# Seven block products instead of eight for three more pairs of column chunks per layer, in a two-layer hybrid mixer

## The chip, the cores and the metric

The kernel runs on one core of one Trainium2 chip. The metric is the device time in microseconds (us). Three runs of the kernel before took 2103.38, 2103.51 and 2104.88 us; their median is 2103.51 us.

## The reference, cut to what matters

Each of two layers multiplies the 256 tokens (width 2048) by one wide matrix `w_in`, splits the result into the inputs of four branches A, B, C, D and the gates, runs four attentions, and merges. All is float32.

```python
for l in range(DEPTH):                                   # 2 layers
    h = jnp.einsum('bsd,de->bse', x, w_in[l])            # 256 tokens x 2048 -> D_IN columns
    (aq, ak, av, az, bq, bk, bv, bz, cq, ck, cv, cz, dq, dk, dv, dz, gl) = _split(h, IN_SIZES)
    ya, yb, yc, yd = ...                                 # differential, neighbourhood, axial GQA, dilated attention
    ys = jnp.stack([ya * silu(az), yb * silu(bz), yc * silu(cz), yd * silu(dz)], axis=2)
    proj = jnp.einsum('bsnw,nwd->bsnd', ys, w_branch[l])
    gates = sigmoid(gl + b_gate)                         # 4 branches x 2048 columns
    merged = jnp.sum(proj * gates, axis=2)
    x = layer_norm(ALPHA * x + merged @ w_out[l])
```

## The kernel before

**Products.** The transposed activations lie in SBUF (the core's working memory) as a high part `th` and a low part `tl` (both in the tile `tx`). Weights come by DMA in groups of two 128-row blocks (`load_raw`, L140), and are split into a high part by ScalarE (`whi`, L150) and a low part by VectorE (`wlo`, L151). Each block product is three matmuls: low times high, high times high, high times low. `whl` holds four groups of split weights, so the splits can run up to some groups ahead of TensorE.

**Chunks.** `chunk` (L195 to L199) multiplies all 2048 rows by one chunk of up to 512 columns: eight groups of two blocks, each for both halves of the tokens, 12 matmuls a group and 96 a chunk. `chunk_t` (L222, L223) makes a part of 256 columns transposed, 64 matmuls in four groups; branch D's queries and keys come that way, two parts to a call of `pairs`. After a part, `fold` copies one half of each sum out of PSUM (the accumulator banks) on ScalarE (`fo`, L231) and adds the other on VectorE (L235), and `rotate` applies the rotary factors: two copies on ScalarE (`xs`, L330), three operations on VectorE (L332 to L334). `xs` lies in a scratch tile with the tag `rb`.

**Seven products.** The gate columns already go by pairs of chunks. For the first four of the 16 row blocks, taken as a 2x2 arrangement (two token halves by two groups of rows) against two groups of rows by two chunks, `gate_pair` makes the result from seven block products instead of eight. It needs sums of activations, `sh` and `sl`, which `quarter_sums` makes once per layer: a sum `xq` (tag `ra`), four sums `xf` (tag `rb`), and their split into `sh` (ScalarE) and `sl` (VectorE). It also adds raw weights to each other (L864), and keeps partial results in `keep` (tag `ra`) and `part` (tag `rb`). It uses all four banks of the pool `psw`.

**Order.** `step()` advances the attention tasks by one stage after every group, so their small matmuls (scores `sc`, transposes `pt`, values `po`) lie between the groups. In a layer: columns of A, `quarter_sums`, columns of B, gates of branch 0, columns of C (chunk `Cz`, then two units `Cqkv0` and `Cqkv1`), gates of branch 1, columns of D, gates of branches 2 and 3, output product. In D each head's values (`Dv0` to `Dv3`, 384 columns) come after the queries and keys it needs, and the head's attention is queued after its values. The framework sets each engine's order when the program is built; on the chip each engine goes through its list in order.

Of the kernel before, what the change touches and what calls it, by code (L numbers as in the profile page):

```python
# [17 lines left out]
P = 128  # L18
# [76 lines left out]
def hybrid_encoder(ctx: ExitStack, tc: tile.TileContext, a: dict, out: bass.AP):  # L95
# [579 lines left out]
    for l in range(DEPTH):  # L675
# [45 lines left out]
        def cols_t(nm, part):  # L721
            return chunk_t(w_in, OFFSETS[nm] + part * D * TCH)

        def v_tile():
            return att.tile([P, 1024], F32, tag="v", name="v")[:, :768].rearrange("p (t n) -> p t n", t=2)

        def columns_ab(br):
            zs, ysT = new_branch()
            for u in range(2):
                v = v_tile()  # L730
                first = (br, u) == ("A", 0)
                if first and l == 0:
                    with tc.manual_schedule(engines={mybir.EngineType.PE, mybir.EngineType.Activation, mybir.EngineType.DVE, mybir.EngineType.SP}):
# [8 lines left out]
                        sw.extend(small_weights())  # L742
                neglam, sg, gn, bias = sw
                for half in range(2):
                    nc.vector.tensor_copy(v[:, half, 0:256], ps[half][:, 0:256])
# [15 lines left out]

        def columns_c():
            zs, ysT = new_branch()
            ps = cols("Cz")
            for half in range(2):
                silu2(ps[half], zs[:, half])
            for u in range(2):
                qk, v = qkT_tile(3, F32).rearrange("p (t n) -> p t n", t=2), v_tile()
                ps = cols(f"Cqkv{u}")
                for half in range(2):  # L770
                    nc.scalar.copy(qk[:, half, 0:384], ps[half][:, 0:384])
                    nc.vector.tensor_copy(v[:, half, 0:128], ps[half][:, 384:512])
                tasks.append(attend_c(u, qk, v, zs, ysT, sw[2]))
            return ysT

        def columns_d():
            zs, ysT = new_branch()
            mask_d = cst.tile([P, 768], F32, tag="bias", name="mask_d")
            nc.sync.dma_start(out=mask_d, in_=a["mask_d"])
            ps = cols("Dz", True)  # L780
            for half in range(2):
                silu2(ps[half], zs[:, half])
            table = [rope_d[:, i].unsqueeze(1).to_broadcast([64, 2, 2, P]) for i in range(2)]
            ready = []
# [12 lines left out]
            heads = []  # L797
            for h in range(4):
                while len(ready) < 3 * h + 3:
                    pairs(len(ready) // 2)  # L800
                v = v_tile()
                for half, ps in enumerate(cols(f"Dv{h}", True)):
                    nc.vector.tensor_copy(v[:, half], ps)
                tasks.append(attend_d(h, heads[h], v, zs, ysT, mask_d))
            return ysT

        def merged_t(c):
# [9 lines left out]
            merged_t(3)  # L817
            yield

        def quarter_sums():  # L820
# [4 lines left out]
            (a11, a12), (a21, a22) = ([x[:, j * KG:(j + 1) * KG, i * P:(i + 1) * P] for j in range(2)] for i in range(2))  # L825
# [4 lines left out]
        def product(bank, lh, ll, w, start=False, stop=False):  # L830

            hi, lo = w
            for k in range(KG):
                nc.tensor.matmul(bank, lhsT=ll[k], rhs=hi[:, k], start=start and k == 0, stop=False, skip_group_check=True)  # L834
                nc.tensor.matmul(bank, lhsT=lh[k], rhs=hi[:, k], start=False, stop=False, skip_group_check=True)  # L835
            for k in range(KG):
                nc.tensor.matmul(bank, lhsT=lh[k], rhs=lo[:, k], start=False, stop=stop and k == KG - 1, skip_group_check=True)  # L837

        def plain(half, g):
            return [[tok(t, g * KG + k, half, False) for k in range(KG)] for t in (th, tl)]  # L840

        def summed(i):
            return [[t[:, i, k] for k in range(KG)] for t in (sh, sl)]

        def gate_pair(b, cp):


            c1, c2 = 2 * cp + 1, 2 * cp
            bgs = []
            for c in (c1, c2):  # L850
# [3 lines left out]
            bg1, bg2 = bgs  # L854
            size = P * KG * NCH

            def raw(c, g):
                return load_raw(w_in, OFFSETS[f"G{b}{c}"] + g * size, KG * NCH)

            def bank():  # L860
                return psw.tile([P, NCH], F32, tag="pw", name="pw")

            def add(out, x, y, op=ALU.add):
                nc.vector.tensor_tensor(out=out, in0=x, in1=y, op=op)  # L864

            def gate(t):
                g = vec.tile([P, NCH], F32, tag="g", bufs=3, name="g")
                nc.scalar.activation(out=g, in_=t, func=AF.Tanh, scale=0.5)
                return g

            def tmp():
                return vec.tile([P, NCH], F32, tag="tmp", bufs=3, name="gt")

            def rest(c, g, p0, p1, first=False):

                w = split_w(raw(c, g), NCH)
                product(p1, *plain(1, g), w, first, g == NK // KG - 1)
                product(p0, *plain(0, g), w, False, g == NK // KG - 1)
                step()

            keep = att.tile([P, 2, NCH], F32, tag="ra", name="keep", bufs=1)
            part = att.tile([P, 2, NCH], F32, tag="rb", name="part", bufs=1)
            r11, r12, r21 = raw(c1, 0), raw(c2, 0), raw(c1, 1)
            pa = bank()
            product(pa, *plain(0, 0), split_w(r11, NCH), True)
            add(r11, r11, r12)
            add(keep[:, 0], pa, bg1)
            pd = bank()
            product(pd, *summed(0), split_w(r11, NCH), True)
            add(keep[:, 1], pd, bg2)  # L890
            pb = bank()
            product(pb, *plain(0, 1), split_w(r21, NCH), True)
            step()
            r22 = raw(c2, 1)
            pe = bank()
            rest(c2, 2, pd, pe, True)
            add(r11, r11, r22)
            product(pa, *summed(1), split_w(r11, NCH))
            add(part[:, 0], pa, bg2, ALU.subtract)
            step()  # L900
            rest(c2, 3, pd, pe)
            add(r12, r12, r22)
            product(pa, *summed(2), split_w(r12, NCH))
            add(part[:, 1], pa, keep[:, 1], ALU.subtract)
            rest(c2, 4, pd, pe)
            add(r11, r11, r21)
            product(pa, *plain(1, 1), split_w(r11, NCH))
            step()
            rest(c2, 5, pd, pe)
            product(pd, *summed(3), split_w(r22, NCH))  # L910
            rest(c2, 6, pd, pe)
            rest(c2, 7, pd, pe)
            ts = [tmp(), tmp()]
            add(ts[1], pe, part[:, 1], ALU.subtract)
            add(ts[0], pd, part[:, 0], ALU.subtract)
            gs = [gate(t) for t in ts]
            rest(c1, 2, pb, pa)
            rest(c1, 3, pb, pa)
            yield gs
            for g in range(4, NK // KG):  # L920
                rest(c1, g, pb, pa)
            ts = [tmp(), tmp()]
            add(ts[1], pa, bg1)
            add(ts[0], pb, keep[:, 0])
            yield [gate(t) for t in ts]

        def gates(b, ysT, first):
            yh, yl = ysT
# [15 lines left out]
                            nc.vector.tensor_tensor(out=merged[:, half, cs], in0=merged[:, half, cs], in1=t, op=ALU.add)  # L944

        pending = {}

        def drain_for(b):
            want = pending.pop(b)
# [146 lines left out]
```

## Time and profile before

| | |
|---|---|
| median of 3 runs | 2103.51 us |
| the profiled execution | 2104.6 us, of which the span of the program is 2102.8 us |
| TensorE matmuls (PE) | 2084.4 us busy, 99% of the span, 10384 matmuls |
| TensorE weight loads (PEld) | 1767.7 us, 84% |
| VectorE (DVE) | 1479.4 us, 70% |
| ScalarE (ACT) | 1045.7 us, 50% |
| GpSimd (POOL) | 38.3 us, 2% |
| DMA | 410.78 MB, mean 195 GB/s |
| share of PE in the chain that ended last | 96% |

Busy time is the union of an engine's instructions. A matmul's own duration is longer than its turn on the engine, since matmuls overlap: the turn is read from the distance of their starts in the timeline. The time of a timeline row with several instructions runs from the first one's start to the last one's end.

### The profile page before, as it was taken

The numbers are of one execution on the slowest core, as the hardware profiler recorded it, in microseconds if no ns is written. First come the engines' busy times: TensorE is split into PE (matmuls) and PEld (weight loads), VectorE is DVE, ScalarE is ACT, GpSimd is POOL, SyncE is SP. The second block draws the span as 40 slices with busy tenths as digits, with TensorE's granted clock in tenths as the row PEclk, the third lists the DMA queues.
The fourth block names the chain that finished last, engine by engine and source line by source line (L and its number), as shares of the span: only waits on it lengthen the run. The fifth ranks groups of instructions, "written<-read, shape, count | busy, mean of one in ns | idle before, by whom it ended". The sixth has DMA issues, their size and how long they took to land.

```text
span 2102.8 us, 27473 instructions
## 1 busy us (share of the span) xinstructions
PE 2084.4 (99%) x10384; PEld 1767.7 (84%) x10384; DVE 1479.4 (70%) x1823; ACT 1045.7 (50%) x1385; POOL 38.3 (2%) x34
## 2 busy tenths in 40 slices
PE   8999999999999999999999999999999999999997
PEld 6888888888898988888888888888889999888886
DVE  6777775877666677776676777657766666777766
ACT  6664554544555554444446545445445454544542
POOL 2000000000000010000000000000000000000000
PEclk9999999999999999999999999999999999999999
DMA  8567666556555566666665545755655554666664
GB/s 272 170 197 239 203 201 199 190 186 213 161 181 164 177 229 207 220 211 216 201 216 180 173 142 189 243 188 191 205 189 181 176 162 149 220 210 215 212 212 126
DMA packets 121603, 410.78 MB, mean 195 GB/s; under 512 B 13888, under 2 KB 14912, under 8 KB 120960
## 3 DMA queue, kind: packets, MB, share of 16 engines
q1 hardware_dynamic: 120608, 407.98, 59.6%
q8 instruction: 81, 1.33, 0.3%
q10 hardware_dynamic: 864, 1.07, 0.2%
q14 instruction: 50, 0.41, 0.1%
HBM read 402.70 MB, written 6.29 MB: 195 GB/s over the span
## 4 chain that ended last, share of the span: by engine, by line
PE 96%; DVE 1%; DMA 1%; ACT 0%; issue 0%; SPq 0%; ACTq 0%; DVEq 0%
PE pw L222 14%; PE pw L195 12%; PE pw L196 12%; PE pw L199 12%; PE pw L837 11%; PE pw L834 11%; PE pw L835 11%; PE pw L223 7%; PE pt L296 1%; PE po L451 1%; PE po L523 1%; PE sc L509 1%; DVE wlo L151 0%; PE sc L383 0%; DMA lnr<-in_emb_ln_g 0%; PE pt L812 0%
## 5 line engine op out<-in xcount | busy, mean ns | idle before, releaser
L151 DVE TENSOR_TENSOR wlo<-wraw,whi 128x1024 fp32r<-128x1024 f32 (+1 forms) x768 | 917.0, 1203 | 486.0 <-ACT whi L150 482.0
L150 ACT CAST whi<-wraw 128x1024 fp32r<-128x1024 f32 (+1 forms) x768 | 789.6, 1033 | 871.2 <-PE pw L196 301.9
L222 PE MATMUL pw<-tx,whi 128*128 128x512 f32 x1280 | 458.0, 401 | 0.0
L195 PE MATMUL pw<-whi,tx 128*128 128x512 f32 (+1 forms) x944 | 358.1, 379 | 0.4 <-DVE tx L241 0.4
L223 PE MATMUL pw<-tx,wlo 128*128 128x256 f32 x1280 | 358.4, 280 | 0.0
L196 PE MATMUL pw<-whi,tx 128*128 128x512 f32 (+1 forms) x944 | 354.5, 376 | 0.0
L834 PE MATMUL pw<-whi,tx 128*128 128x512 f32 x864 | 339.0, 392 | 0.0
L835 PE MATMUL pw<-whi,tx 128*128 128x512 f32 x864 | 336.6, 390 | 0.0
L222 PEld LDWEIGHTS pw<-tx,whi 128*128 128x128 f32 x1280 | 240.4, 188 | 55.2
L199 PE MATMUL pw<-wlo,tx 128*128 128x512 f32 (+1 forms) x944 | 277.9, 375 | 0.0
L837 PE MATMUL pw<-wlo,tx 128*128 128x512 f32 x864 | 265.9, 390 | 0.0
L223 PEld LDWEIGHTS pw<-tx,wlo 128*128 128x128 f32 x1280 | 241.7, 189 | 0.4
L195 PEld LDWEIGHTS pw<-whi,tx 128*128 128x128 f32 x944 | 179.3, 190 | 27.4 <-DVE tx L241 0.6
L196 PEld LDWEIGHTS pw<-whi,tx 128*128 128x128 f32 x944 | 179.3, 190 | 25.8
L199 PEld LDWEIGHTS pw<-wlo,tx 128*128 128x128 f32 x944 | 176.4, 190 | 27.5
L837 PEld LDWEIGHTS pw<-wlo,tx 128*128 128x128 f32 x864 | 161.3, 188 | 36.2 <-DVE wlo L151 2.1
L834 PEld LDWEIGHTS pw<-whi,tx 128*128 128x128 f32 x864 | 162.3, 188 | 32.8
L835 PEld LDWEIGHTS pw<-whi,tx 128*128 128x128 f32 x864 | 162.3, 188 | 32.8
L195 PE MATMUL pw<-whi,yl 128*128 128x512 f32 x256 | 100.2, 391 | 0.0
L196 PE MATMUL pw<-whi,yh 128*128 128x512 f32 x256 | 99.7, 389 | 0.0
L199 PE MATMUL pw<-wlo,yh 128*128 128x512 f32 x256 | 79.5, 391 | 0.0
L864 DVE TENSOR_TENSOR wraw<-wraw 128x1024 f32<-128x1024 f32 x64 | 78.0, 1219 | 0.8
(174 smaller groups left out, 1660.1 us busy)
## 6 DMA issues: line engine op xcount, KB each, us to landing
wraw<-in_w_in SPq DMA_DIRECT2D x544, 512.0 KB, 4.2
wraw<-in_w_branch SPq DMA_DIRECT2D x64, 512.0 KB, 4.8
wraw<-in_w_out SPq DMA_DIRECT2D x64, 512.0 KB, 4.3
wraw<-in_w_in SPq DMA_DIRECT2D x64, 384.0 KB, 3.1
bg<-in_b_gate SPq DMA_DIRECT2D x32, 256.0 KB, 4.9
xr<-x_dram SPq DMA_DIRECT2D x16, 256.0 KB, 4.7
bias<-in_rpb SPq DMA_DIRECT2D x2, 1024.0 KB, 7.2
x_dram<-merged SPq DMA_DIRECT2D x8, 256.0 KB, 4.9
```

The lines of the kernel that those rows point to most:

```text
L150: nc.scalar.copy(hi[:, :w], raw)
L151: nc.vector.tensor_tensor(out=lo[:, :w], in0=raw, in1=hi[:, :w].bitcast(F32), op=ALU.subtract)
L195: nc.tensor.matmul(acc[half][:, :n], lhsT=tok(ll, k, half, perm), rhs=hi[:, kk, :n], start=k == 0, stop=False)
L196: nc.tensor.matmul(acc[half][:, :n], lhsT=tok(lh, k, half, perm), rhs=hi[:, kk, :n], start=False, stop=False)
L199: nc.tensor.matmul(acc[half][:, :n], lhsT=tok(lh, k, half, perm), rhs=lo[:, kk, :n], start=False, stop=k == nkt - 1)
L222: nc.tensor.matmul(acc[b], lhsT=hi[:, kk, cs], rhs=tx[:, k].rearrange("p h t -> p (h t)"), start=k == 0, stop=False)
L223: nc.tensor.matmul(acc[b][:, SEQ:], lhsT=lo[:, kk, cs], rhs=th[:, k, :], start=False, stop=k == NK - 1)
L296: nc.tensor.transpose(pt[:, q * P:(q + 1) * P], src[:, q * P:(q + 1) * P], ident)
L834: nc.tensor.matmul(bank, lhsT=ll[k], rhs=hi[:, k], start=start and k == 0, stop=False, skip_group_check=True)
L835: nc.tensor.matmul(bank, lhsT=lh[k], rhs=hi[:, k], start=False, stop=False, skip_group_check=True)
L837: nc.tensor.matmul(bank, lhsT=lh[k], rhs=lo[:, k], start=False, stop=stop and k == KG - 1, skip_group_check=True)
L864: nc.vector.tensor_tensor(out=out, in0=x, in1=y, op=op)
```

## The change

Three more pairs of chunks per layer go through the seven products: `Cz` with `Cqkv0`, `Dv0` with `Dv1`, and `Dv2` with `Dv3`. The body of `gate_pair` becomes `seven`, with the bias as an option; without one, three evacuations per pair are ScalarE copies instead of VectorE additions (`kept`, L880 of the new file). Branch D takes its token halves as even and odd tokens, so the sums are made anew in that order at the start of D (`quarter_sums(True)`), and back in the plain order at its end (`quarter_sums()`). `drain_to(1)` advances the queued attention until one task is left. The values of a pair of heads now come together, after the queries and keys of the first of them. Calls before in D: pairs 0, 1, `Dv0`, pairs 2, `Dv1`, pairs 3, 4, `Dv2`, pairs 5, `Dv3`. Calls now: sums, pairs 0, 1, `Dv0` and `Dv1`, pairs 2, pairs 3, 4, `Dv2` and `Dv3`, pairs 5, sums. What follows in both is the gates of branch 2.

```diff
 def columns_c():
-    ps = cols("Cz")
+    both = cols_pair("Cz", "Cqkv0")
+    ps = next(both)
...
-        ps = cols(f"Cqkv{u}")
+        ps = cols("Cqkv1") if u else next(both)
 def columns_d():
+    quarter_sums(True)
     ps = cols("Dz", True)
...
     for h in range(4):
         while len(ready) < 3 * h + 3:
             pairs(len(ready) // 2)
-        v = v_tile()
-        for half, ps in enumerate(cols(f"Dv{h}", True)):
-            nc.vector.tensor_copy(v[:, half], ps)
-        tasks.append(attend_d(h, heads[h], v, zs, ysT, mask_d))
+        if h % 2 == 0:
+            both = cols_pair(f"Dv{h}", f"Dv{h + 1}", True)
+            vs = []
+        for ps in both:
+            drain_to(1)
+            vs += v_tiles(1, 384)
+            for half in range(2):
+                nc.vector.tensor_copy(vs[-1][:, half], ps[half])
+            if h % 2 == 0 and len(vs) == 1:
+                tasks.append(attend_d(h, heads[h], vs[0], zs, ysT, mask_d))
+        if h % 2:
+            tasks.append(attend_d(h, heads[h], vs[1], zs, ysT, mask_d))
+    quarter_sums()
     return ysT
 -def quarter_sums():
+def quarter_sums(perm=False):
...
+def seven(raw, n, perm=False, bias=None):
...
+    def kept(out, x, i, op=ALU.add):
+        if bias:
+            add(out, x, bias[i], op)
+        else:
+            nc.scalar.copy(out, x)
...
+    r11, r12, r21 = raw(1, 0), raw(0, 0), raw(1, 1)
+    pa = bank()
+    product(pa, *plain(0, 0), split_w(r11, n), True)
+    add(r11, r11, r12)
+    kept(keep[:, 0], pa, 1)
+    pd = bank()
+    product(pd, *summed(0), split_w(r11, n), True)
+    kept(keep[:, 1], pd, 0)
+    pb = bank()
+    product(pb, *plain(0, 1), split_w(r21, n), True)
...
```

**First place: TensorE where branch D ends and the gates of branch 2 begin, layer 0.** Before, the last chunk is `Dv3`; `pw_6651` and `pw_6664` are the banks of the gate pair's first and second product, `pw_6676` that of the third, and `sc_6687` holds head 3's first scores.

```order
L199 MATMUL pw_6480<-wlo_6622,tx_98 128x384 x2
...
L835 MATMUL pw_6651<-whi_6652,tx_98 128x512
L837 MATMUL pw_6651<-wlo_6653,tx_98 128x512 x2
...
L834 MATMUL pw_6664<-whi_6665,sl_101 128x512
L835 MATMUL pw_6664<-whi_6665,sh_100 128x512
L837 MATMUL pw_6664<-wlo_6666,sh_100 128x512 x2
...
L837 MATMUL pw_6676<-wlo_6678,tx_98 128x512 x2
L509 MATMUL sc_6687<-qkT_6068 128x256
L509 MATMUL sc_6687<-qkT_6068 128x128 x2
```

Now the last matmuls of D are those of the last part of pairs 5 (bank `pw_6577`). `pw_6710`, `pw_6723` and `pw_6735` are the first, second and third product's banks, `sc_6746` head 3's first scores, `pt_6792` the transposes of its softmax.

```order
L223 MATMUL pw_6577<-tx_98,wlo_6659 128x256
...
L863 MATMUL pw_6710<-whi_6711,tx_98 128x512
L865 MATMUL pw_6710<-wlo_6712,tx_98 128x512 x2
L509 MATMUL sc_6746<-qkT_6099 128x256
L509 MATMUL sc_6746<-qkT_6099 128x128 x2
L296 MATMUL pt_6792<-ident_87,pr_6754 128x128 x4
L862 MATMUL pw_6723<-whi_6724,sl_101 128x512
L863 MATMUL pw_6723<-whi_6724,sh_100 128x512
...
L865 MATMUL pw_6735<-wlo_6737,tx_98 128x512 x2
```

The scores and the transposes moved ahead of the second product, and the 96 matmuls of `Dv3` that stood between pairs 5 and the gates are gone from there. Layer 1 has the same order.

**The same place on VectorE.** Before, from the copy of the last values on:

```order
L803 COPY v_6478<-pw_6480 128x384
L864 TENSOR_TENSOR keep_6643<-pw_6651,bg_6639 128x512
L151 TENSOR_TENSOR wlo_6706<-wraw_6703,whi_6705 128x1024
L864 TENSOR_TENSOR keep_6643<-pw_6664,bg_6641 128x512
L864 TENSOR_TENSOR wraw_6645<-wraw_6645,wraw_6700 128x1024
L512 SCALAR_TENSOR_TENSOR scb_6691<-sc_6687,mask_d_4399 128x512
L283 TENSOR_REDUCE nm_6693<-scb_6691 128x1
```

Now, from the second-last split before the rotation of pairs 5's last part (`qkT_6099`) to the low part of the sums, which the second product reads:

```order
L151 TENSOR_TENSOR wlo_6782<-wraw_6704,whi_6781 128x1024
L874 TENSOR_TENSOR wraw_6704<-wraw_6704,wraw_6708 128x1024
L332 TENSOR_TENSOR qkT_6099<-qkT_6099,rope_d_94 64x512
L333 TENSOR_TENSOR xs_6683<-xs_6683,rope_d_94 64x512
L334 TENSOR_TENSOR qkT_6099<-qkT_6099,xs_6683 64x512
L848 TENSOR_TENSOR xf_6690<-xq_6689 128x256 x2
L848 TENSOR_TENSOR xf_6690<-xf_6690,xq_6689 128x256
L512 SCALAR_TENSOR_TENSOR scb_6750<-sc_6746,mask_d_4402 128x512
L848 TENSOR_TENSOR xf_6690<-xf_6690,xq_6689 128x256
L283 TENSOR_REDUCE nm_6752<-scb_6750 128x1
L874 TENSOR_TENSOR keep_6702<-pw_6710,bg_6700 128x512
L241 TENSOR_TENSOR sl_101<-xf_6690,sh_100 128x1024
```

The rotation, the four sums, the softmax of head 3 and the evacuation of the first product stand in one line ahead of `sl_101`, none of which was there before.

**Second place: ScalarE where `Dv2` begins, layer 0.** Before: `fo` and `xs` belong to the last part of pairs 4, the casts to 768 columns are `Dv2`'s.

```order
L231 COPY fo_5967<-pw_5865 128x256
L150 CAST whi_6048<-wraw_6046 128x1024
L231 COPY fo_5967<-pw_5866 128x256
L330 COPY xs_5972<-qkT_5725 32x512 x2
L150 CAST whi_6085<-wraw_6083 128x768
L150 CAST whi_6103<-wraw_6101 128x768
```

Now, with `keep` from the first (`pw_6119`) and the second product (`pw_6132`):

```order
L231 COPY fo_6100<-pw_6009 128x256
L150 CAST whi_6160<-wraw_6158 128x768
L231 COPY fo_6100<-pw_6010 128x256
L150 CAST whi_6177<-wraw_6113 128x768
L880 COPY keep_6111<-pw_6119 128x384
L150 CAST whi_6190<-wraw_6188 128x768
L330 COPY xs_6105<-qkT_6099 32x512 x2
L880 COPY keep_6111<-pw_6132 128x384
```

The copies of the first products out of PSUM are new on ScalarE here, and the second one stands behind two casts and the rotation's copies. Where `Dv0` begins, and in layer 1, the order is the same.

## Rows read from the trace of the kernel before

**Rows 1.** The page: busy time of TensorE, and the chain by engine.
```profile
PE 2084.4 (99%) x10384; PEld 1767.7 (84%) x10384; DVE 1479.4 (70%) x1823; ACT 1045.7 (50%) x1385; POOL 38.3 (2%) x34
...
PE 96%; DVE 1%; DMA 1%; ACT 0%; issue 0%; SPq 0%; ACTq 0%; DVEq 0%
```
**Rows 2.** Timeline, TensorE, `Dv0` of layer 0, first and last (start us, us, instruction).
```profile
575.57 0.34 PE L195 MATMUL pw<-whi,tx 128*128 128x384 f32 x1
...
591.87 0.51 PE L199 MATMUL pw<-wlo,tx 128*128 128x384 f32 x2
```
**Rows 3.** Timeline, TensorE, the output chunks of layer 0, first and last.
```profile
969.87 0.48 PE L195 MATMUL pw<-whi,tx 128*128 128x512 f32 x1
...
1053.85 0.62 PE L199 MATMUL pw<-wsp,tx 128*128 128x512 f32 x2
```
**Rows 4.** Groups by form: busy us, mean ns, idle before.
```profile
L834 PE MATMUL pw<-whi,tx 128*128 128x512 f32 x864 | 339.0, 392 | 0.0
...
L290 ACT ACTIVATE pr<-scb,nm 128x512 f32<-128x512 f32 x16 | 11.6, 723 | 28.5 <-DVE nm L283 28.5
...
L512 DVE SCALAR_TENSOR_TENSOR scb<-sc,mask_d 128x512 f32<-128x512 f32 x16 | 11.0, 689 | 11.2 <-PE sc L509 11.1
...
L771 ACT COPY qkT<-pw 128x384 f32<-128x384 f32 x8 | 3.8, 477 | 2.9 <-PE pw L199 2.9
```
**Rows 5.** Timeline, three engines, end of pairs 5 in layer 0.
```profile
727.41 0.28 PE L223 MATMUL pw<-tx,wlo 128*128 128x256 f32 x1
...
727.65 0.83 ACT L150 CAST whi<-wraw 128x768 fp32r<-128x768 f32 x1 [0.94 <-PE pw L222]
...
728.87 0.38 ACT L231 COPY fo<-pw 128x256 f32<-128x256 f32 x1
...
729.40 0.42 DVE L235 TENSOR_TENSOR qkT<-pw,fo 128x256 f32<-128x256 f32 x1
...
729.85 1.25 ACT L330 COPY xs<-qkT 32x512 f32<-32x512 f32 x2 [0.60 <-DVE qkT L235]
...
731.13 0.68 DVE L332 TENSOR_TENSOR qkT<-qkT,rope_d 64x512 f32<-64x512 f32 x1 [1.31 <-ACT xs L330]
...
732.34 0.94 DVE L151 TENSOR_TENSOR wlo<-wraw,whi 128x768 fp32r<-128x768 f32 x1
...
733.21 0.68 DVE L334 TENSOR_TENSOR qkT<-qkT,xs 64x512 f32<-64x512 f32 x1
```
**Rows 6.** Timeline, the shortest rotation in D and the longest in A.
```profile
552.28 0.28 PE L223 MATMUL pw<-tx,wlo 128*128 128x256 f32 x1
...
557.34 0.67 DVE L334 TENSOR_TENSOR qkT<-qkT,xs 64x512 f32<-64x512 f32 x1
...
65.12 0.28 PE L223 MATMUL pw<-tx,wlo 128*128 128x256 f32 x1
...
73.74 0.69 DVE L334 TENSOR_TENSOR xr<-xr,xs 128x512 f32<-128x512 f32 x1
```
**Rows 7.** Timeline, VectorE and ScalarE, the sums of layer 0 after branch A.
```profile
125.94 1.22 DVE L824 TENSOR_TENSOR xq<-tx 128x1024 f32<-128x1024 f32 x1
...
127.19 0.76 DVE L827 TENSOR_TENSOR xf<-xq 128x256 f32<-128x256 f32 x2
...
129.86 1.05 ACT L240 CAST sh<-xf 128x1024 fp32r<-128x1024 f32 x1
...
131.14 1.22 DVE L241 TENSOR_TENSOR sl<-xf,sh 128x1024 fp32r<-128x1024 f32 x1
```
**Rows 8.** Stretches at the end: us, busy us (instructions) of each engine, granted clock, DMA.
```profile
2091.50:2095.00 3.50, 0.28 (x2) 0.00 (x0) 3.08 (x7) 0.00 (x0) 0.99 (x1) 1.00 0.00 0
2095.00:2099.00 4.00, 0.00 (x0) 0.00 (x0) 4.00 (x7) 0.00 (x0) 0.00 (x0) 0.51 0.37 131
```
**Rows 9.** Stretches at the start, the transposes into the tile idle alone (TensorE, weight loads).
```profile
1.34:5.34 4.00, 4.00 (x19) 4.00 (x20) 1.00 0.77 228
6.34:8.34 2.00, 1.92 (x18) 1.68 (x16) 1.00 1.10 363
```

More of the change, by code (lines that the diff above doesn't have):

```diff
@@ L722, in cols_t, with v_tiles, cols_pair @@
             return chunk_t(w_in, OFFSETS[nm] + part * D * TCH)
-        def v_tile():
-            return att.tile([P, 1024], F32, tag="v", name="v")[:, :768].rearrange("p (t n) -> p t n", t=2)
+        def v_tiles(units, n):
+            v = att.tile([P, 1024], F32, tag="v", name="v")
+            return [v[:, u * 2 * n:(u + 1) * 2 * n].rearrange("p (t n) -> p t n", t=2) for u in range(units)]
+        def cols_pair(one, other, perm=False):
+            n = len(CHUNKS[one])
+            return seven(lambda i, g: load_raw(w_in, OFFSETS[(one, other)[i]] + g * P * KG * n, KG * n), n, perm)
         def columns_ab(br):
@@ L828, in quarter_sums @@
             split_evac(sh, sl, f)
[L830 to L843, printed above, removed]
+        def seven(raw, n, perm=False, bias=None):
+            def bank():
+                return psw.tile([P, NCH], F32, tag="pw", name="pw")[:, :n]
+            def product(bank, lh, ll, w, start=False, stop=False):
+                hi, lo = w
+                for k in range(KG):
+                    nc.tensor.matmul(bank, lhsT=ll[k], rhs=hi[:, k], start=start and k == 0, stop=False, skip_group_check=True)
+                    nc.tensor.matmul(bank, lhsT=lh[k], rhs=hi[:, k], start=False, stop=False, skip_group_check=True)
+                for k in range(KG):
+                    nc.tensor.matmul(bank, lhsT=lh[k], rhs=lo[:, k], start=False, stop=stop and k == KG - 1, skip_group_check=True)
+            def plain(half, g):
+                return [[tok(t, g * KG + k, half, perm) for k in range(KG)] for t in (th, tl)]
+            def summed(i):
+                return [[t[:, i, k] for k in range(KG)] for t in (sh, sl)]
+            def add(out, x, y, op=ALU.add):
+                nc.vector.tensor_tensor(out=out, in0=x, in1=y, op=op)
+            def kept(out, x, i, op=ALU.add):
[3 more added lines that the diff above has]
+                    nc.scalar.copy(out, x)
+            def rest(i, g, p0, p1, first=False):
+                w = split_w(raw(i, g), n)
+                product(p1, *plain(1, g), w, first, g == NK // KG - 1)
+                product(p0, *plain(0, g), w, False, g == NK // KG - 1)
+                step()
+            keep = att.tile([P, 2, NCH], F32, tag="ra", name="keep", bufs=1)[:, :, :n]
+            part = att.tile([P, 2, NCH], F32, tag="rb", name="part", bufs=1)[:, :, :n]
+            r11, r12, r21 = raw(1, 0), raw(0, 0), raw(1, 1)
[8 more added lines that the diff above has]
+            product(pb, *plain(0, 1), split_w(r21, n), True)
+            step()
+            r22 = raw(0, 1)
+            pe = bank()
+            rest(0, 2, pd, pe, True)
+            add(r11, r11, r22)
+            product(pa, *summed(1), split_w(r11, n))
+            kept(part[:, 0], pa, 0, ALU.subtract)
+            step()
+            rest(0, 3, pd, pe)
+            add(r12, r12, r22)
+            product(pa, *summed(2), split_w(r12, n))
+            add(part[:, 1], pa, keep[:, 1], ALU.subtract)
+            rest(0, 4, pd, pe)
+            add(r11, r11, r21)
+            product(pa, *plain(1, 1), split_w(r11, n))
+            step()
+            rest(0, 5, pd, pe)
+            product(pd, *summed(3), split_w(r22, n))
+            rest(0, 6, pd, pe)
+            rest(0, 7, pd, pe)
+            add(part[:, 1], pe, part[:, 1], ALU.subtract)
+            add(part[:, 0], pd, part[:, 0], ALU.subtract)
+            rest(1, 2, pb, pa)
+            rest(1, 3, pb, pa)
+            yield [part[:, 0], part[:, 1]]
+            for g in range(4, NK // KG):
+                rest(1, g, pb, pa)
+            if bias:
+                add(keep[:, 1], pa, bias[1])
+            add(keep[:, 0], pb, keep[:, 0])
+            yield [keep[:, 0], keep[:, 1] if bias else pa]
@@ L871, in tmp @@
[L871 to L925, printed above, removed]
+            for ts in seven(lambda i, g: load_raw(w_in, OFFSETS[f"G{b}{2 * cp + i}"] + g * size, KG * NCH), NCH, bias=bgs):
+                gs = []
+                for half in (1, 0):
+                    g = vec.tile([P, NCH], F32, tag="g", bufs=3, name="g")
+                    nc.scalar.activation(out=g, in_=ts[half], func=AF.Tanh, scale=0.5)
+                    gs.insert(0, g)
+                yield gs
@@ L946, in hybrid_encoder, with drain_to @@
         pending = {}
+        def drain_to(n):
+            while len(tasks) > n:
+                step()
         def drain_for(b):
```

27 lines of the change are left out of this document (8 added, 19 removed).

## The prediction

> **What bounds the kernel now.** I read the page first. TensorE is busy for 2084.4 of 2102.8 us and makes up 96% of the chain that ended last, while VectorE is at 70% and ScalarE at 50% [rows 1]. The groups by form come next: the matmuls of the gate pairs, which already use seven products, show no idle time before them [rows 4]. So every turn on TensorE that goes is time saved, every wait of TensorE that comes is time lost, and work on the other engines costs nothing until TensorE waits for it. The rest of the reading is therefore of two kinds: what a matmul's turn is worth (timeline of TensorE), and how long the hand-overs take at the places where the change puts a TensorE instruction close behind what it needs (timeline of VectorE and ScalarE, beside the new order).
>
> **The matmuls removed.** A pair of chunks had eight block products of six matmuls for its first quarter and now has seven, so six go per pair. One pair per layer has 512 columns, two have 384. In `Dv0` 94 turns lie between the two rows' starts: (591.87 - 575.57) / 94 = 0.173 us for 384 columns [rows 2]. Of the 384 matmuls of the output chunks the last 372 stand in a row, with 370 turns between the rows shown: (1053.85 - 969.87) / 370 = 0.227 us for 512 columns [rows 3]. Saved: 2 x 6 x 0.227 + 4 x 6 x 0.173 = 2.7 + 4.2 = 6.9 us.
>
> **The added work on VectorE and ScalarE.** A pair gets three more weight splits, four weight sums and some additions or copies; a layer gets two more sets of activation sums. This is roughly 30 us of VectorE a layer, beside about 310 us of idle time there. I cost it at nothing except at the two places below: the gate pairs carry the same load and TensorE does not wait in them [rows 4]. If that cover were gone at the start of D, where the first new set of sums lies, it would cost at most the set itself, 1.2 + 4 x 0.4 + 1.2, about 4 us a layer; nothing reads those sums until `Dv0`, two calls of pairs later, so I take 0. The weight transfers are the same in number and size, and of the six buffers for raw weights four stay held at the head of a pair as in the gate pairs, so they too are costed at nothing. For `Cz` with `Cqkv0` I take 0 too: same width as a gate pair, and the copies stand right behind the products.
>
> **First place: the end of D.** Here `Dv3` used to stand between the last rotation and the gates; its 96 matmuls, 16.6 us at 0.173, covered the rotation. Now pairs 5 is followed at once by the gate pair, and in TensorE's order the first product comes, then head 3's scores, the transposes of its softmax, and only then the second product, which reads `sh` and `sl`. What they need hangs in one line on the end of the last matmul of pairs 5; call that T.
>
> - In the trace T is 727.41 + 0.28 = 727.69, and the second copy, the second addition, the `xs` copies and the three rotary operations end at 733.21 + 0.68, T + 6.2 [rows 5]. The shortest such line in D ends 5.45 us after its T, 558.01 against 552.56, and the longest in A, where more splits stand between, 9.03 us, 74.43 against 65.40 [rows 6].
> - In the new order a 1024-column cast stands ahead of the second copy, so that the addition ends at about T + 2.6 (T + 2.1 in the trace) and `xs` 1.25 later, about T + 4.0. VectorE has a split and a weight sum ahead of the rotation, about 1.2 each (the row of `sl` is of the same size and kind) [rows 7], which end at T + 4.9. Two operations at 0.6 (731.13 to 732.34 is two of them) and the third at 0.7, with no split between, end at T + 6.8.
> - Then three of the four sums `xf` (two take 0.76, so 0.34 a turn) to T + 7.8 [rows 7]; the masked scores, 0.6 to 0.7 [rows 4], to T + 8.4; the last sum to T + 8.8; `sh` on ScalarE, 1.05, to T + 9.9, beside the row maximum and the evacuation of the first product, 0.6 each, on VectorE; `sl`, 1.22, to T + 11.2 [rows 7]. The exponential, 0.72 [rows 4], follows `sh` and the transposes end before `sl`. The second product starts at about T + 11.3.
> - TensorE has work of its own in that time: the first product, 6 x 0.227 = 1.4, and scores and transposes, eight blocks of 128 columns at 0.11, 0.9 [rows 9]. It loses 11.3 - 2.3 = 9.0 us per layer. With the shortest rotation it is 7.7, with the longest 11.3. I take 9.0, next to the row in the same place, and two layers make 18.0.
>
> **The clock after it.** From T + 1.8 to T + 6.8 TensorE has nothing to do, and little until T + 11.3. [...] At the start TensorE begins after idling, and does 19 transposes in 4.0 us, then 18 in 2.0 us [rows 9]: the first stretch of work ran at half pace (its clock column says 1.00, so I go by the pace). So it stays at half pace for between 4.0 us (to 5.34) and 5.0 us (to 6.34), and loses half of that, 2.0 to 2.5. I take 2.3 per layer, 4.6 for both; ends 0 and 2.5 each. [...]
>
> **Second place: the starts of `Dv0` and `Dv2`.** Each begins right behind a part whose rotation still runs. Three products and half a group, 24 x 0.173 = 4.2 us, and two matmuls more lie ahead of the first matmul that adds to the second product's bank, so TensorE arrives at T + 4.5. That bank must have been copied into `keep`. ScalarE has ahead of that copy: two casts at 0.83 and the second `fo` at 0.38 [rows 5], the first `keep` copy at 0.48 [rows 4], a third cast, and the `xs` copies, 1.25, which wait for an addition on VectorE anyway: 4.6 us from T, with the copy itself 5.1. Lost 0.8 with the hand-over, four times 3.2. Between 0, if the casts were done earlier, and 1.5, with VectorE's addition one split (0.94) later [rows 5].
>
> **Sum, against the profiled execution.** 2104.6 - 6.9 + 18.0 + 4.6 + 3.2 = 2123.5. The median of the runs is 1.1 below that execution, so I predict 2122.4 us.
>
> **Rivals.**
> - *The wait without the clock.* The scores, the transposes and the first product might keep the clock up, in the middle of the program, where it has run at full rate for long. Then 2122.4 - 4.6 = 2117.8. For it: there is some work inside the gap. Against it: five microseconds of it have none. Chance 0.27.
> - *Not slower: the line is covered.* If TensorE did the third product and the next group while the second waits, or the sums were ready in time, only the saving and the second place would count: 2103.5 - 6.9 + 3.2 = 2099.8. The deciding point is a loss of (6.9 - 3.2) / 2 = 1.85 us per layer, a second product that starts by T + 4.1. Against it: the `xs` copies alone end at T + 3.4 in the trace [rows 5], and six operations follow. [...] Chance 0.05: 2099.8 lies just inside the bound for no change below, so 0.03 of it counts as that and 0.02 as faster.
> - *More waits than these.* If the starts of `Dv0` and `Dv2` ran dry of splits, since VectorE has a 768-column weight sum beside nearly every split there, each would lose not 0.8 but some 4 us, four weight sums of 0.95: 2122.4 + 4 x 3.2 = 2135. Against it: gate pairs do the same with wider weights and do not wait [rows 4], though no rotation stands in theirs. Chance 0.08.
>
> **Chances and range.** The forecast has 0.60. The low end takes the shortest rotation, no fall of the clock and no loss at the second place: 2103.5 - 6.9 + 2 x 7.7 = 2112.0. The high end takes the longest rotation, 2.5 of clock and 1.5 at each start: 2103.5 - 6.9 + 22.6 + 5.0 + 6.0 = 2130.2. I give 2111 to 2131. No change means within 0.2%, 4.2 us, about what a measurement of this kernel can tell. Faster by more: 0.02 and the same: 0.03, from the covered line, and 0.01 more of the same from a forecast whose every term falls short; slower: 0.94.
>
> **What would show it.** Right: the count of matmuls falls by 36; TensorE has one gap of some 9 us in all per layer just behind the first product of branch 2's gates, ended by `sl`, with `sh` and the rotation before it in the chain of waits; the granted clock falls there; and small gaps at `Dv0` and `Dv2` end with the `keep` copy on ScalarE. Wrong: no idle time of TensorE there, or the second product waiting for something that is not in this line, such as a weight transfer; or gaps in `Cz`, where I have none.

## The result, and the profile after

The changed kernel takes 2122.25 us (median of 4 runs, 2122.02 to 2123.68); the kernel before takes 2103.45 us (median of 4, 2103.34 to 2104.88). The ratio is 1.0089, 95% interval 1.0077 to 1.0101: slower by 18.8 us. The prediction was 2122.4 us.

The page of the changed kernel: its span, the busy time by engine, and the chain by engine.

```profile
span 2121.9 us, 27531 instructions
...
PE 2085.5 (98%) x10348; PEld 1765.3 (83%) x10348; DVE 1544.3 (73%) x1913; ACT 1069.1 (50%) x1425; POOL 38.3 (2%) x34
...
PE 87%; issue 7%; DVE 3%; ACT 2%; DMA 1%; POOL 0%; SPq 0%; ACTq 0%; DVEq 0%; POOLq 0%
```

The matmuls fell from 10384 to 10348, the 36 forecast, and yet TensorE's busy time rose by 1.1 us [rows 1]: some of the matmuls that are left run slower. TensorE's share of the last chain fell from 96% to 87%; "issue" and VectorE came in. That share alone does not measure the loss: a kernel below that is faster than the kernel before (early sums in the shared scratch) has 88%, and 7% "issue", too. The view of waits (the waiting engine, tile and line; who releases it; us in total, times, longest) names the places:

```profile
PE sc L509 <- DVE qkT L334: 9.8, 2, 4.9
PE pt L296 <- ACT pr L290: 6.1, 2, 3.1
...
PE pt L307 <- DVE qkT L490: 1.2, 2, 0.6
PE pw L862 <- ACT keep L880: 0.8, 4, 0.2
PE pt L343 <- DVE ys L525: 0.5, 1, 0.5
```

The first two lines are the end of D, once per layer; the third is the start of D; the fourth the starts of `Dv0` and `Dv2`. Layer 0's end of D, in a timeline of TensorE, VectorE and ScalarE (start us, us, instruction, idle time before and what ended it):

```profile
743.25 0.28 PE L223 MATMUL pw<-tx,wlo 128*128 128x256 f32 x1
743.37 0.40 PE L862 MATMUL pw<-whi,tx 128*128 128x512 f32 x1
...
744.77 0.81 PE L509 MATMUL sc<-qkT 128*128 128x256 f32 x4
...
746.17 1.25 ACT L330 COPY xs<-qkT 32x512 f32<-32x512 f32 x2 [0.41 <-DVE qkT L235]
747.30 1.22 DVE L874 TENSOR_TENSOR wraw<-wraw 128x1024 f32<-128x1024 f32 x1
748.45 0.68 DVE L332 TENSOR_TENSOR qkT<-qkT,rope_d 64x512 f32<-64x512 f32 x1
...
749.76 0.68 DVE L334 TENSOR_TENSOR qkT<-qkT,xs 64x512 f32<-64x512 f32 x1
750.48 0.76 DVE L848 TENSOR_TENSOR xf<-xq 128x256 f32<-128x256 f32 x2
750.50 0.79 PE L509 MATMUL sc<-qkT 128*128 128x128 f32 x2 [4.91 <-DVE qkT L334]
...
752.54 1.05 ACT L240 CAST sh<-xf 128x1024 fp32r<-128x1024 f32 x1 [5.12 <-DVE xf L848]
...
753.62 1.23 DVE L241 TENSOR_TENSOR sl<-xf,sh 128x1024 fp32r<-128x1024 f32 x1
...
754.35 1.11 PE L296 MATMUL pt<-ident,pr 128*128 128x128 f32 x4 [3.07 <-ACT pr L290]
...
755.12 0.77 PE L862 MATMUL pw<-whi,sl 128*128 128x512 f32 x1
```

Before, the second product followed the first at once (timeline of TensorE, first and second product):

```profile
745.77 0.39 PE L834 MATMUL pw<-whi,tx 128*128 128x512 f32 x1
...
747.16 0.39 PE L834 MATMUL pw<-whi,sl 128*128 128x512 f32 x1
```

T, the end of the last matmul of pairs 5, is 743.25 + 0.28 = 743.53. The rotation (L334) ends at 750.44, T + 6.9 (T + 6.2 before [rows 5]); `sl` at 754.85; the second product starts at 755.12, T + 11.6. From the scores' end at 745.58 on, TensorE idles 4.91 and 3.07 us. The first of these waits stands ahead of the last of head 3's scores and is ended by the rotation. The view puts the second wait down to the softmax (`pr`), which ends beside `sl`: both stand behind the same rotation. The third product waits as well, though it needs nothing of the sums: it starts at 757.83, behind the second. By their lines, all 10348 matmuls of this trace start in the built order.

The same place in stretches (us; busy us and instructions of TensorE, weight loads, VectorE, ScalarE, GpSimd; granted clock; DMA):

```profile
743.53:748.00 4.47, 2.05 (x10) 1.53 (x9) 4.25 (x5) 3.46 (x5) 0.00 (x0) 1.00 0.27 80
748.00:751.00 3.00, 0.51 (x2) 0.50 (x2) 2.93 (x6) 0.00 (x0) 0.00 (x0) 0.75 0.57 194
751.00:755.12 4.12, 1.05 (x6) 0.77 (x5) 3.91 (x8) 1.76 (x3) 0.00 (x0) 0.50 0.07 27
755.12:759.76 4.64, 4.64 (x13) 3.66 (x12) 1.69 (x2) 1.63 (x2) 0.00 (x0) 0.50 0.00 0
```

VectorE is busy 4.25 + 2.93 + 3.91 of the 11.6 us: the wait is a line of work on VectorE. The granted clock goes from 1.00 to 0.50 at 749.52, 3.9 us after the scores' end, and back to 1.00 at 759.76; before, it fell only at the program's end [rows 8]. Here 4.64 us of dense products run at the clock of 0.50: a turn of 512 columns takes 0.43 us (755.69 to 756.12) where it takes 0.23 behind 759.76. By an estimate from the clock the stretch loses half its length, 2.3 us. Layer 1 shows the same, 0.50 from 1797.41 to 1807.65.

Where the time went comes from the first matmul of each PSUM bank in both traces, as the growth of after minus before from one bank to the next (us, both layers together):

| | forecast | measured |
|---|---|---|
| start of the run, branch A | 0 | -1.0 |
| `Cz` pairs | -2.7 | -2.8 |
| start of D, first new sums | 0 | +1.6 |
| D pairs: removed matmuls and waits at their starts | -4.2 + 3.2 | -1.4 |
| end of D to the second pair of branch 2's gates: wait and clock | wait 18.0 + clock 4.6 | layer 0 11.5 + layer 1 11.3 = 22.8 |
| the rest, to the end (with the 0.5 of wait at L343 in layer 0) | 0 | 0 |
| sum, of the span | 18.9 | 19.2; the spans differ by 19.1 |

The start of D, which was costed at nothing (timeline, VectorE and TensorE, layer 0):

```profile
518.14 0.55 DVE L490 TENSOR_TENSOR qkT<-ra,rb 128x384 f32<-128x384 f32 x1
...
518.75 0.66 PE L307 MATMUL pt<-ident,qkT 128*128 128x128 f32 x4 [0.61 <-DVE qkT L490]
```

Before (the same two instructions):

```profile
512.30 0.55 DVE L490 TENSOR_TENSOR qkT<-ra,rb 128x384 f32<-128x384 f32 x1
...
519.70 0.60 PE L307 MATMUL pt<-ident,qkT 128*128 128x128 f32 x4
```

A norm and rotation of branch C runs on VectorE there between the new sums and the splits. Its last step (L490) used to be done 6.9 us ahead of the transposes that need it; now they wait for it and come 0.6 to 0.8 us late. The busy share does not tell this: from 500 to 510 us VectorE was busy for 9.57 us here and for 9.96 us before. At `Dv0` (timeline, ScalarE and TensorE), as forecast, the second copy stands behind `xs`:

```profile
577.03 1.25 ACT L330 COPY xs<-qkT 32x512 f32<-32x512 f32 x2
...
578.31 0.48 ACT L880 COPY keep<-pw 128x384 f32<-128x384 f32 x1
...
578.84 0.45 PE L862 MATMUL pw<-whi,tx 128*128 128x384 f32 x1 [0.20 <-ACT keep L880]
```

Against the turns before it, this matmul and the next start 0.37 + 0.11 us late: 0.5 where 0.8 was forecast, four times.

### The profile page after: what moved, and what is told of

The parts are those of the page before. It is cut to its first block, busy times and chain, and to the rows that moved or that the text cites. A ratio compares the mean times of both kernels' runs of the same rounds, so it can differ in the third digit from the quotient of the medians.

```text
span 2121.9 us, 27531 instructions
## 1 busy us (share of the span) xinstructions
PE 2085.5 (98%) x10348; PEld 1765.3 (83%) x10348; DVE 1544.3 (73%) x1913; ACT 1069.1 (50%) x1425; POOL 38.3 (2%) x34
## 4 chain that ended last, share of the span: by engine, by line
PE 87%; issue 7%; DVE 3%; ACT 2%; DMA 1%; POOL 0%; SPq 0%; ACTq 0%; DVEq 0%; POOLq 0%
PE pw L222 14%; PE pw L862 12%; PE pw L863 12%; PE pw L865 12%; PE pw L195 8%; PE pw L199 8%; PE pw L196 8%; PE pw L223 7%; DVE wlo L151 1%; PE pt L296 1%; ACT whi L150 1%; PE po L523 1%; PE sc L509 1%; PE po L451 1%; PE sc L383 0%
## 5 line engine op out<-in xcount | busy, mean ns | idle before, releaser
L151 DVE TENSOR_TENSOR wlo<-wraw,whi 128x1024 fp32r<-128x1024 f32 (+1 forms) x786 | 935.9, 1202 | 436.7 <-ACT whi L150 432.9
L150 ACT CAST whi<-wraw 128x1024 fp32r<-128x1024 f32 (+1 forms) x786 | 801.4, 1031 | 840.1 <-PE pw L863 259.6
L862 PE MATMUL pw<-whi,tx 128*128 128x512 f32 (+1 forms) x1188 | 455.6, 384 | 0.8 <-ACT keep L880 0.8
L863 PE MATMUL pw<-whi,tx 128*128 128x512 f32 (+1 forms) x1188 | 452.2, 381 | 0.0
L865 PE MATMUL pw<-wlo,tx 128*128 128x512 f32 (+1 forms) x1188 | 354.7, 380 | 0.0
L862 PEld LDWEIGHTS pw<-whi,tx 128*128 128x128 f32 x1188 | 225.0, 189 | 40.9 <-ACT keep L880 2.1
L863 PEld LDWEIGHTS pw<-whi,tx 128*128 128x128 f32 x1188 | 225.1, 190 | 37.0
L865 PEld LDWEIGHTS pw<-wlo,tx 128*128 128x128 f32 x1188 | 222.7, 189 | 38.5
L195 PE MATMUL pw<-whi,tx 128*128 128x512 f32 x560 | 221.0, 395 | 0.4 <-DVE tx L241 0.4
L196 PE MATMUL pw<-whi,tx 128*128 128x512 f32 x560 | 218.8, 391 | 0.0
L199 PE MATMUL pw<-wlo,tx 128*128 128x512 f32 x560 | 173.3, 390 | 0.0
L195 PEld LDWEIGHTS pw<-whi,tx 128*128 128x128 f32 x560 | 105.5, 188 | 22.3 <-DVE tx L241 0.6
L199 PEld LDWEIGHTS pw<-wlo,tx 128*128 128x128 f32 x560 | 105.3, 188 | 22.4
L196 PEld LDWEIGHTS pw<-whi,tx 128*128 128x128 f32 x560 | 105.6, 189 | 20.9
L874 DVE TENSOR_TENSOR wraw<-wraw 128x1024 f32<-128x1024 f32 (+1 forms) x88 | 102.9, 1169 | 0.6
```

What stands on the lines that cost most here:

```text
L150: nc.scalar.copy(hi[:, :w], raw)
L151: nc.vector.tensor_tensor(out=lo[:, :w], in0=raw, in1=hi[:, :w].bitcast(F32), op=ALU.subtract)
L195: nc.tensor.matmul(acc[half][:, :n], lhsT=tok(ll, k, half, perm), rhs=hi[:, kk, :n], start=k == 0, stop=False)
L196: nc.tensor.matmul(acc[half][:, :n], lhsT=tok(lh, k, half, perm), rhs=hi[:, kk, :n], start=False, stop=False)
L199: nc.tensor.matmul(acc[half][:, :n], lhsT=tok(lh, k, half, perm), rhs=lo[:, kk, :n], start=False, stop=k == nkt - 1)
```

## The experiments

In each the kernel before ran beside on the same chip (medians 2103.56, 2103.91 and 2103.66 us for the three groups of runs). Ratios are to that, with 95% intervals.

**Early sums in their own scratch.** The plain-order sums are made right behind `Dv2`, `Dv3`, ahead of pairs 5, in tiles that the rotation does not use; none are made at the end.

```diff
+                if h == 2:
+                    early_sums()      # same sums, tags g and bc instead of ra and rb, in two halves
                 if h % 2:
                     tasks.append(attend_d(h, heads[h], vs[1], zs, ysT, mask_d))
-    quarter_sums()
     return ysT
```

> The sums in the plain order are made in scratch of their own, right behind the values of heads 2 and 3 and ahead of the last call of pairs; all else is as in the changed kernel. Theory (the wait of the second product for sums whose scratch is freed only by the last rotation, and the clock after it, cost about 12 us per layer): the wait and the fall of the clock go, 2122.3 - 24 = 2098.3 us, at most 1 us of idle TensorE at the place. Rival (head 3's rotation and softmax are the wait, and the sums only stand beside it): TensorE waits for the rotation all the same, some 5 us per layer stay, 2108 to 2113 us.

Measured: 2099.68 us, ratio 0.9978 (0.9969 to 0.9987), 1.4 us above the theory's time. Timeline of TensorE, first product, second, and the scores that used to stand between:

```profile
742.51 0.40 PE L877 MATMUL pw<-whi,tx 128*128 128x512 f32 x1
...
743.92 0.40 PE L877 MATMUL pw<-whi,sl 128*128 128x512 f32 x1
...
746.66 0.81 PE L509 MATMUL sc<-qkT 128*128 128x256 f32 x4
```

The second product follows after 1.41 us, which is six matmuls, and the granted clock is 1.00 from 730 to 760 us, with TensorE busy for all 30.00. The time is 22.6 us below the changed kernel's by the medians, and 25.3 by the spans of the profiled executions (the slowest of four there, the fastest of ten here, so the medians count); the table has 22.8 at this place and 1.6 at the start of D, whose wait is gone here too (below). So the wait and its clock were more than the whole of the loss.

Two orders changed with this edit, though. The sums stand earlier on VectorE, and the framework also put head 3's scores behind the second and third products on TensorE. In the changed kernel they stand ahead of the second product, and TensorE waits 4.91 us there for the rotation, which early sums alone would not take away. So the rival's time did not come, but its mechanism was not tried: no run has early sums with the scores left in their old place.

**All queries and keys ahead of the last values.** Pairs 5 comes before `Dv2` and `Dv3`, so that their matmuls cover the last rotation; the sums stay at the end.

```diff
-        while len(ready) < 3 * h + 3:
+        while len(ready) < (12 if h > 1 else 3 * h + 3):
```

> The last call of pairs stands ahead of the values of heads 2 and 3, so that these cover the rotation; the sums stay at the end, in the shared scratch. Theory: the rotation leaves the line, which is now evacuation, sums and split: about 7 us from the last matmul to the second product, of which TensorE has 3 us of work: 4 us lost per layer, and the clock may just hold: 2106 us, 2111 us if it falls. Rival (sums alone are the wait, the rotation had been hidden): as the changed kernel, 2120 to 2122 us. The other rival (the rotation alone is the wait): 2098 us.

Measured: 2118.14 us, ratio 1.0065 (1.0051 to 1.0079). A miss: only 4.1 us came back. Timeline, VectorE and TensorE:

```profile
742.49 0.35 DVE L819 COPY v<-keep 128x384 f32<-128x384 f32 x1
...
743.02 1.21 DVE L844 TENSOR_TENSOR xq<-tx 128x1024 f32<-128x1024 f32 x1
...
747.33 0.80 PE L296 MATMUL pt<-ident,pr 128*128 128x128 f32 x4 [3.89 <-ACT pr L290]
...
748.42 1.21 DVE L241 TENSOR_TENSOR sl<-xf,sh 128x1024 fp32r<-128x1024 f32 x1
...
750.14 0.77 PE L862 MATMUL pw<-whi,sl 128*128 128x512 f32 x1
```

The rotation is out of the line, but its place is taken: the values' partial results are held in the same scratch (`keep` in `ra`, `part` in `rb`), and the sums start as soon as their last copy is made (742.49, then `xq` at 743.02). `sl` ends at 749.63, and the second product starts 10.0 us after the first (740.12). So taking the rotation out of the line gave back about a fifth of the loss. The sums still begin behind whatever used the scratch last, and head 3's softmax still stands ahead of the second product on TensorE; this run does not part the two.

**The same sums early, in the shared scratch.** Only the call moves. (With the call left at the end and scratch of its own, the framework builds the same program as for the early sums in their own scratch: that run stands for both.)

```diff
+                if h == 2:
+                    quarter_sums()
...
-    quarter_sums()
```

> The plain-order sums of branch D's end keep their shared scratch (ra, rb) and are made by the same function; only the call moves, from the end of D to right behind the values of heads 2 and 3, ahead of pairs 5. Theory (what costs is the sums' place behind the last rotation, however they got there): the second product of branch 2's gates follows the first by about 1.4 us as with scratch of their own, the clock does not fall in mid-program, and the time is that of the kernel with early sums in their own scratch, 2099.7 us (2099 to 2100.5). Rival (the shared scratch itself costs: the sums hold rb until sl is done, so the rotation of pairs 5 that follows, which needs rb for its copies, comes late and the gates wait for TensorE's scores again): some 1 to 3 us per layer more, 2102 to 2106.

Measured: 2101.46 us, ratio 0.999 (0.9981 to 0.9998). Timeline of TensorE, start of D, first and second product:

```profile
518.67 0.33 PE L307 MATMUL pt<-ident,qkT 128*128 128x128 f32 x1 [0.60 <-DVE qkT L490]
...
743.26 0.40 PE L863 MATMUL pw<-whi,tx 128*128 128x512 f32 x1
...
744.67 0.40 PE L863 MATMUL pw<-whi,sl 128*128 128x512 f32 x1
```

The second product follows after 1.41 us again, so the theory holds where it speaks and the rival falls. The shared scratch may stay if the call moves, and the call may stay if the scratch is its own, since the framework then moves the sums itself. Here too head 3's scores come behind the second and third products (first scores at 747.41), so the 20.8 us between this kernel and the changed one belong to both orders together. The time lies 1.8 above that of the scratch of its own, outside what was expected. Of that the wait at the start of D, 0.77 us per layer against the usual turn, makes 1.5 (the profiled executions differ by 3.1; the other 1.6 of that stays open); with own scratch the wait at the start of D is absent:

```profile
516.36 0.55 DVE L490 TENSOR_TENSOR qkT<-ra,rb 128x384 f32<-128x384 f32 x1
...
517.28 0.60 PE L307 MATMUL pt<-ident,qkT 128*128 128x128 f32 x4
```

(timeline of the kernel with early sums in their own scratch). There the built order has C's norm two splits earlier on VectorE, and L490 ends 1.8 us sooner. That the order makes the difference is read from the two traces; no run changed it alone.

**Only branch C by seven products.** D is as before the change, without new sums.

```diff
-    quarter_sums(True)
...
-        if h % 2 == 0:
-            both = cols_pair(f"Dv{h}", f"Dv{h + 1}", True)
+        for half, ps in enumerate(cols(f"Dv{h}", True)):
...
-    quarter_sums()
```

> Only the pair of C goes through seven products; branch D and the sums are as before the change. Theory: 2 x 6 matmuls of 0.227 us, 2103.5 - 2.7 = 2100.8 us. Rival (the ScalarE copies and the second user of the banks cost as much as is saved): 2103 to 2104 us.

Measured: 2100.37 us, ratio 0.9985 (0.9976 to 0.9994): 3.2 us less than before, where 2.7 was worked out. In its trace the `Cz` pairs gain 2.8, and the rest lies ahead of them, as in the changed kernel. This part of the change pays as counted.

**Idle transposes in the gap.** 40 transposes into the tile `idle` behind the first product at the end of D; then, in a second kernel, 44 there and 28 more behind head 3's scores. The edit in outline (`dummy(n)` issues n transposes):

```diff
     product(pa, *plain(0, 0), split_w(r11, n), True)
+    if fill:                            # first pair of branch 2's gates only
+        dummy(40)                       # transposes of ident; second kernel: 44
...
     product(pb, *plain(0, 1), split_w(r21, n), True)
     step()
+    if fill:                            # second kernel only
+        dummy(28)
```

> The changed kernel with 40 idle transposes of 128 columns behind the first product at the end of D, which write a tile that nothing reads: TensorE has 4.4 us of work in its wait. Theory (the granted clock falls in the wait and costs 2.3 us per layer beyond it): the clock stays up and the wait itself stays, 2122.3 - 4.6 = 2117.7 us. Rival (the clock costs nothing there, since the line that TensorE waits for runs on other engines): 2122 us, or a little more if the transposes delay the scores.

> As e4_fill, but with 44 idle transposes behind the first product and 28 more behind head 3's scores, so that TensorE has work through nearly the whole wait (after e4_fill's 40 the granted clock still fell, about 3 us after the last of them). Theory (the fall of the clock costs 2.3 us per layer beyond the wait): no stretch at 0.5 in mid-program, the wait itself as before, 2122.3 - 4.6 = 2117.7 us. Rival (the clock costs nothing beyond the wait): 2122 us with the clock at 1.0 throughout.

Measured: 2122.3 us (ratio 1.0085, 1.0071 to 1.0098) with 40, and 2118.63 us (1.0066, 1.0052 to 1.008) with 44 and 28. Stretches of the first, then of the second:

```profile
748.00:751.79 3.79, 1.92 (x14) 1.48 (x11) 3.72 (x9) 0.00 (x0) 0.00 (x0) 1.00 0.37 138
751.79:754.37 2.58, 0.54 (x3) 0.29 (x3) 2.58 (x5) 1.76 (x3) 0.00 (x0) 0.50 0.00 0
754.37:758.62 4.25, 4.25 (x11) 3.38 (x11) 1.30 (x3) 1.04 (x1) 0.00 (x0) 0.50 0.00 0
```

```profile
745.00:751.00 6.00, 6.00 (x51) 5.66 (x49) 5.75 (x8) 2.64 (x5) 0.00 (x0) 1.00 0.40 117
751.00:756.00 5.00, 4.58 (x37) 4.14 (x37) 4.53 (x10) 2.08 (x4) 0.00 (x0) 1.00 0.17 70
```

The first did not hold the clock: it fell to 0.50 at 751.79, some 1.3 us after the last scores, so it says nothing of the price. The second did, and its second product still starts at T + 11.4 (T = 744.17, second product at 755.54). So the wait is not the clock's doing, and the clock's price is 2122.25 - 2118.63 = 3.6 us by the medians, 2121.9 - 2117.1 = 4.8 by the spans of the profiled executions; 4.6 was forecast. The rival without the clock's fall (2117.8 us) describes this kernel, not the changed one.

**The copies on VectorE.** Early sums in their own scratch, and:

```diff
-            nc.scalar.copy(out, x)
+            nc.vector.tensor_copy(out, x)
```

> e1_early_sums with the copies of the first products out of PSUM on VectorE instead of ScalarE, in C and D. Theory (at the start of Dv0 and Dv2 TensorE waits 0.5 us for the second copy, which stands behind casts and the rotation's copies on ScalarE): four waits of 0.5 us go, 2099.7 - 1.9 = 2097.8 us. Rival (VectorE, with weight sums and the rotation, is no earlier): 2099.7 us or 1 to 3 us more.

Measured: 2097.8 us, ratio 0.997 (0.9958 to 0.9981), 1.9 us less than with the copies on ScalarE. Timeline of TensorE at `Dv0`, where the wait stood:

```profile
578.22 0.51 PE L880 MATMUL pw<-wlo,tx 128*128 128x384 f32 x2
578.56 0.34 PE L877 MATMUL pw<-whi,sl 128*128 128x384 f32 x1
...
579.63 0.34 PE L877 MATMUL pw<-whi,tx 128*128 128x384 f32 x1
```

No idle time is left; 4 x 0.48 = 1.9 agrees. The spans of the profiled executions (2096.6 with the copies on ScalarE, 2097.0 here) would not show it: the first was the fastest of its ten, and this one waits 1.0 us beside a GpSimd operation (last section). In the shared scratch the same edit gives:

> The moved call of the run beside it, and the kept copies of the pairs without a bias on VectorE in place of ScalarE. Theory: the waits at the starts of Dv0 and Dv2 (0.37 + 0.11 us, four times) go as they went with the sums in their own scratch, so 1.9 us less than the run beside it, 2097.8 us. Rival (VectorE, which now has the copies beside the sums in the shared scratch, is late for a split somewhere): no less than the run beside it, 2099.7 us.

Measured: 2099.26 us, ratio 0.9979 (0.997 to 0.9988): 2.2 less than its partner, about as the theory says.

**The sums of D behind `Dz`.** Early sums in their own scratch, and the permuted sums made after `Dz` instead of before it, to take away the wait at the start of D; then the same with the copies on VectorE.

```diff
-    quarter_sums(True)
     ps = cols("Dz", True)
     for half in range(2):
         silu2(ps[half], zs[:, half])
+    quarter_sums(True)
```

> e1_early_sums with the sums in the order of D made behind Dz instead of ahead of it. Theory (those sums delay branch C's second unit on VectorE, and TensorE waits 0.8 us per layer for its rotation ahead of a transpose): the wait goes, 2099.7 - 1.6 = 2098.1 us. Rival (VectorE is full there, and what goes in one place comes in the next): 2099.7 us, with a gap later in D.

> f1_sums_after_z and f2_keep_vector together. Theory: the two do not meet, 2099.7 - 1.6 - 1.9 = 2096.2 us. Rival: VectorE carries both more copies and the sums at the start of D, and one of the two gains is lost, 2098 us.

Measured: 2100.17 us (ratio 0.998, 0.9972 to 0.9989) and 2098.09 us (0.997, 0.9959 to 0.9981): no gain over the kernels with the sums before `Dz`, 2099.68 and 2097.8. The expectation missed because its premise was wrong: with scratch of their own, that wait was no longer there to be taken away. Between these two the copies on VectorE are worth 2.1 us again.

The fastest version is early sums in their own scratch with the copies on VectorE, 2097.8 us: 6.1 us below the kernel before beside it (2103.91), 24 below the changed one.

## Why the prediction was right

- *Removed matmuls, -6.9.* Right: 36 fewer, the `Cz` pairs gain 2.8 in the trace and 3.2 alone.
- *First place, wait.* Right in mechanism and size. The forecast had the rotation's end at T + 6.8 and the second product at T + 11.3, the trace T + 6.9 and T + 11.6. One link was late: the transposes, forecast to be done before `sl`, ran at the clock of 0.50, and the second product started 0.27 us after `sl` ended. The line was right as built, but its links were not equally to blame: taking the rotation out alone gave back 4.1 us, moving the sums, and with them head 3's scores, gave back all of it.
- *The clock, 4.6.* Right that it falls, in mid-program too, to 0.50 at 749.52 and at 1797.41. Ahead of the result the fall was shown only at the program's end, to 0.51 behind 2095 [rows 8], 3.3 us after the last matmul, and in no gap of mid-program: that it would fall there was the author's estimate. Its price was 3.6 by the medians and 4.8 by single executions, with 4.6 forecast.
- *Second place, 3.2.* Right mechanism, too large: 1.9. At `Dv0` the second copy ended at 578.79, T + 4.7 with T = 574.09, where T + 5.1 was worked out.
- *Added VectorE work at nothing.* Wrong at the start of D, where the prediction named up to 4 us a layer as the loss if uncovered and took 0: it was 0.8 a layer. "Nothing reads those sums until `Dv0`" is true; what was late is other work queued behind them on VectorE. With early sums in their own scratch the same sums cost nothing there, which points to the order on VectorE; no run changed that alone. In `Cz`: no gap, right.
- *The D pairs.* Beyond the waits at their starts they lose some 0.9 us in steps of 0.1 to 0.2, most of them at one head's scores; these were not forecast, and their cause stays open.
- That the sum came within 0.2 us is partly luck: +1.6 at the start of D and +0.9 in the D pairs stand against -1.3 at the second place and -1.0 in branch A and the start. In the last a wait of 0.65 us at a transpose of branch A is gone and TensorE came to its full pace 0.7 us earlier at the start (last section), neither of which the change touches.
- *Rivals.* The covered line falls: TensorE did nothing in the place of the second product. The starts did not run dry of splits.

## What to carry to other kernels

A saving on the bounding engine is worth its turns only if the work that used to lie at that place was not also the cover of something else: before moving a block, list what was late behind it. Work on an engine with time to spare still costs when it stands in one line with a scratch buffer: a temporary that shared its buffer with the last user began only when that user was done (`xf` at 750.48 in the changed kernel, behind the rotation's end at 750.44), and making it earlier, or in another buffer, took back 20.8 and 22.6 us here without taking work away. Such a move can change the other engines' orders too: read them again. When engines are 70% busy on average, look for the few us in which TensorE waits for a line of work on them.

## What the runs showed of the hardware

The clock's fall does not follow from the gap's length alone: with 40 transposes in it, the granted clock fell 1.3 us after TensorE's last scores, in the changed kernel 3.9 us after them, and with 72 it was 1.00 from 745 to 760 us. The start of the program differs from trace to trace too: the first transposes into `idle` start 0.21 us apart and the later ones 0.11, with the step at 6.1 us in the kernel before and at 5.4 us in the changed one, though the clock column says 1.00 throughout.

VectorE's splits take longer beside two GpSimd operations on `bias` (timeline of the fastest kernel):

```profile
772.30 5.75 POOL L707 TENSOR_TENSOR bias<-bias,mask_b 128x1024 f32<-128x1024 f32 x2 [248.62 <-DVE part L889]
772.95 6.18 DVE L151 TENSOR_TENSOR wlo<-wraw,whi 128x1024 fp32r<-128x1024 f32 x2 [0.26 <-ACT whi L150]
...
779.45 0.33 PE L343 MATMUL pt<-ident,ys 128*128 128x128 f32 x1 [1.02 <-DVE ys L525]
```

Two splits take 6.18 us, the second of them 3.42, instead of 2 x 1.2, and TensorE then waits 1.0 us. The second split ends 1.08 us after the GpSimd operation that it started beside (779.13 after 778.05). In the traces of the kernel before and of the changed one the splits that start beside the same two operations end 1.08 to 1.09 us after them as well: 780.80 after 779.71 and 784.16 after 783.07 before, 787.69 after 786.61 and 791.04 after 789.96 in the changed kernel. They take 1.84 and 1.56 us before, 2.33 and 3.24 in the changed kernel, and the wait of TensorE that follows (L343) is 0 before and 0.52 us in the changed kernel.
